# Attention over the paged cache: slots of their own for memory weights and rows, silu moved to a later step, one convolution call left out of step 0

## The chip, the cores and the metric

The kernel runs on one core of a Trainium2 chip. Its metric is the device time of one execution in microseconds (us). The core has five instruction queues that run side by side, each strictly in its own order: PE (matmuls and transposes), DVE (vector), ACT (scalar functions and copies), POOL (a second vector engine, which also issues the gathers) and SP (which issues most transfers). An instruction whose inputs or whose output slot are not ready holds up everything behind it on its queue.

## What is computed

The reference is one step of a decoder layer for a prompt of 1024 rows and for 8 samples of one token each. The stage of this change is the attention of the 8 samples over a paged cache, with other work laid between its matmuls:

```python
def mla_sample(q_nope, q_rope, c_new, kr_new, pool_ckv, pool_krope, page_table, w_uk, w_uv):
    q_lat = jnp.einsum('bthd,lhd->bthl', q_nope, w_uk)             # "absorbed" queries
    past_c = pool_ckv[page_table].reshape(Bd, -1, KV_LORA)         # 4096 cached rows per sample
    past_r = pool_krope[page_table].reshape(Bd, -1, ROPE_DIM)
    s_past = einsum('bthl,bkl->bhtk', q_lat, past_c) + einsum('bthr,bkr->bhtk', q_rope, past_r)
    ...
    p = jax.nn.softmax(s, axis=-1)
    o_lat = einsum('bhtk,bkl->bthl', p[..., :P], past_c) + einsum('bhtk,bkl->bthl', p[..., P:], c_new)

def mem_kv(mem, w_xk, w_xv):            # mem: 256 memory rows; 4 heads of 256 columns
    k = jnp.einsum('bmd,de->bme', mem, w_xk).reshape(B, M, MEM_HEADS, MEM_HEAD_DIM)
    v = jnp.einsum('bmd,de->bme', mem, w_xv).reshape(B, M, MEM_HEADS, MEM_HEAD_DIM)
    return k, v

def conv_tail(y, conv_b, g, b):         # y: causal depthwise convolution with 31 taps
    return jax.nn.silu(layer_norm(y + conv_b, g, b))
```

## The kernel before

Four stages stand ahead (projections and a gated unit, prompt attention), then comes the stage of this change, from about 404 to 680 us of the span, then the output projection, the cross attention over the memory and the feed-forward part.

The stage is a loop of 16 steps: step n works on half e = n % 2 of sample b = n // 2. A step transposes the cached rows on PE (`columns`: eight groups `trc`, then `trr` for the rotary part); the results are copied out of PSUM by ACT and DVE in turn into `ct` (the third and fourth copy of each engine belong to the second half of the groups). Then it multiplies them with the queries (`scores`, tile `main`). After an odd step the softmax of that sample runs in pieces inside the next steps (tiles `mr`, `st`, `mx`, `md`, `ma`, `E_`, `sm`, `sa`), then `values` (tile `pv`) and, behind it, the gathers of a later sample's rows by POOL. In front of all that, in step 0, `absorb` computes the absorbed queries: PE writes `tqs`, `tuk`, twice `tql`, and `tsn`, DVE copies them out as `qT`, `ukT`, `ql` and `SN`. Both `tql` use the one PSUM bank of tag `st`, so the second waits for the copy `ql` of the first. After `absorb` comes `memory_in`, which loads the 256 memory rows in four tiles `min`, transposes them (`trm`) and splits them into a high and a low part (`MH_`, `ML_`).

Three kinds of other work are laid into the steps:

- `memory_kv`: eight products of the memory rows with a head's weights (four heads, keys and values in turn), one product over an odd-even pair of steps (step 1 does a whole one). Each takes its weights in four pieces of 256 KB: a load `kraw` by SP, the high part `kwh` by POOL, the low part `kwl` by DVE, 12 matmuls `mk` on PE. Its result is copied by ACT into `ko`, and SP stores that to memory.
- `convolve`, called four times a step: each call takes `nconv` = 3 of the 62 pieces of the last convolution's DVE chain (`mix<-u,convw,mix`, L354), as long as there are any.
- `norm`, from step 6 on, and the first silu pieces, which activate the first 640 columns of the convolution's output on ACT (eight instructions in all, and the activation table has to be changed ahead of them and back to that of the exponential behind them).

Tiles live in rings of slots: a tag with bufs = 3 gives its tiles three slots in turn, and a tile waits until the last reader of the tile that had its slot is done. Before the change `kraw` and `kwl` share one ring of three; `kwh` and `ko` share one ring of two, so four `kwh` and one `ko` of a product go round it, and the slot of `ko` is taken next but one by the second `kwh` of the next product; it is free when the store of `ko` has landed. `min` has a ring of two.

The order of PE's queue in this stage is the order of the code (`manual_schedule`). The order of the other queues is set by a scheduler from the estimated times at which instructions become ready; `tc.issue_after(x)` holds instructions back until x in that order.

Of the kernel before, what the change touches and what calls it, by code (L numbers as in the profile page):

```python
# [9 lines left out]
F32 = mybir.dt.float32  # L10
F32R = mybir.dt.float32r
# [8 lines left out]
P = 128  # L20
# [5 lines left out]
NT = S + DB  # L26
# [11 lines left out]
MHD = 256  # L38
# [15 lines left out]
CONV_STEPS = 6  # L54
EARLY = 5
# [51 lines left out]
def decoder_step(ctx: ExitStack, tc: tile.TileContext, I: dict, O: dict):  # L107
# [28 lines left out]
    def cast(eng, dst, src):  # L136
        if eng == "a":
            return A.copy(dst, src)  # L138
        if eng == "v":
            return V.tensor_copy(dst, src)  # L140
        return G.tensor_scalar(dst, src, 1.0, 1.0, op0=ALU.mult, op1=ALU.mult)
# [4 lines left out]
    def split(hi, lo, src, he="a", le="v"):  # L146
        return {he: cast(he, hi, src), le: lows(le, lo, src, hi)}

    def mm3(out, lh, ll, rh, rl, start, stop, onto=False):

        T.matmul(out, lh, rh, start=start, stop=False, skip_group_check=onto)  # L151
        T.matmul(out, lh, rl, start=False, stop=False, skip_group_check=onto)  # L152
        T.matmul(out, ll, rh, start=False, stop=stop, skip_group_check=onto)  # L153
# [50 lines left out]
    with ExitStack() as c1:  # L204
# [101 lines left out]
        def glu_w(ct):  # L306
            return load_w([(G0 + ct * P, P), (G0 + CC + ct * P, P)], ct == 0)
# [5 lines left out]
        for ct in range(NCT):  # L313
            wh, wl = w_next if ct == 0 else glu_w(ct)
# [70 lines left out]
        wh, wl = load_w([(C0, LAT + RD)])  # L385
# [29 lines left out]
        for un in range(3):  # L415
            wh, wl = load_w([(un * 256, 256)])
# [40 lines left out]
    def silu(c0, c1):  # L457
        while c0 < c1:
            e = min(c1, c0 + 516)
            for k in range(NCT):  # L460
                v = mixC[:, k, c0:e]
                A.activation(v, v, AF.Silu, bias=cvec[:, 2, k:k + 1], scale=cvec[:, 1, k:k + 1])
            c0 = e


# [184 lines left out]
    with ExitStack() as c2:  # L650
        ps = Banks(tr=3, main=1, st=1, pv=1, mk=1, tl=1)
        pmp = tc.tile_pool(name="pm", bufs=1, side="left", reuse_waits="tile")
        pm = pmp.__enter__()
# [77 lines left out]
        main, probs, cts, krts, tail = {}, {}, {}, {}, {}  # L731
# [105 lines left out]
        def memory_in():  # L837
            for m in range(2):
                for g in range(2):
                    xin = pm.tile([P, 512], F32, tag="min", bufs=2, name="min")  # L840
                    nc.sync.dma_start(xin, I["mem_prompt"][0, m * P:(m + 1) * P, g * 512:(g + 1) * 512])
                    t = ps.tile([P, 4, P], F32, tag=("mk", "main", "pv", "tl")[2 * m + g], name="trm")
                    for k in range(4):
                        T.transpose(t[:, k, :], xin[:, k * P:(k + 1) * P], ident)
                    split(MH_[:, 4 * g:4 * g + 4, m * P:(m + 1) * P], ML_[:, 4 * g:4 * g + 4, m * P:(m + 1) * P], t)

        def memory_kv(h, wname, oname):

            acc = ps.tile([P, 2, MHD], F32, tag="mk", name="mk")
            for q in range(4):  # L850
                raw = pm.tile([P, 2, MHD], F32, tag="kwl", bufs=3, name="kraw")
                wh = pm.tile([P, 2, MHD], F32R, tag="kwh", bufs=2, name="kwh")
                nc.sync.dma_start(raw, I[wname][0, q * 256:(q + 1) * 256, h * MHD:(h + 1) * MHD]
                                  .rearrange("(k p) c -> p k c", p=P))
                wl = pm.tile([P, 2, MHD], F32R, tag="kwl", bufs=3, name="kwl")
                split(wh, wl, raw, "p", "v")
                if q == 2:
                    yield
                for j in range(2):
                    for m in range(2):  # L860
                        k, mc = 2 * q + j, slice(m * P, (m + 1) * P)
                        mm3(acc[:, m, :], MH_[:, k, mc], ML_[:, k, mc], wh[:, j, :], wl[:, j, :],
                            k == 0 and m == 0, k == KD - 1 and m == 1)
            o = pm.tile([P, 2, MHD], F32, tag="kwh", bufs=2, name="ko")
            cast("a", o, acc)
            nc.sync.dma_start(O[oname][0, 0, :, h, :].rearrange("(m p) d -> p m d", p=P), o)

        mkv = [(h, *n) for h in range(MH) for n in (("w_xk", "new_mem_k"), ("w_xv", "new_mem_v"))]
        def run(steps):

            for x in list(steps):
                if next(x, steps) is steps:
                    steps.remove(x)
# [6 lines left out]
        norms = [conv_norm(i, dp, ps, "tl", 2) for i in range(NTL + 1)]  # L880
        rest = conv(NCT - 1, us_[NCT - 1], S // 2)
        nconv = -(-2 * CK // (4 * CONV_STEPS))
        mem, soft, ends = memory_all(), [], []

        def norm():
            if norms and next(norms[0], norms) is norms:
                norms.pop(0)

        def convolve():
            with tc.issue_after(tail["v"].ins):  # L890
                for _ in range(nconv):
                    next(rest, None)

        with tc.manual_schedule(engines={mybir.EngineType.PE}):
            for n in range(2 * DB):
                b, e = divmod(n, 2)
                cols = columns(b, e, n < CONV_STEPS)
                next(cols, None)
                run(soft)
                next(cols, None)  # L900
                run(soft)
                run(ends)
                convolve()
                if n == 0:
                    absorb()
                    memory_in()
                else:
                    next(mem, None)
                if n == 1:
                    next(mem, None)  # L910
                if n > CONV_STEPS:
                    norm()
                run(soft)
                convolve()
                if n >= CONV_STEPS:
                    norm()
                scores(b, e)
                if n == CONV_STEPS + EARLY:
                    with tc.issue_after(tail["a"].ins):
                        silu(0, EARLY * P)  # L920
                convolve()
                if e == 0 and 0 < b < DB - 1:
                    v = values(b - 1)
                    next(v)
                    ends.append(v)
                run(soft)
                convolve()
                if e == 1:
                    soft.append(softmax(b))
                    run(soft)  # L930

            ends = [values(DB - 2)]
            run(ends)
            for _ in range(3):
                run(soft)
            run(ends)
            ends.append(values(DB - 1))
            next(ends[-1])
            run(soft)
            run(ends)  # L940
        assert not norms and not soft and not ends and next(rest, None) is None
        pmp.__exit__(None, None, None)
        rawp.__exit__(None, None, None)
        u3p.__exit__(None, None, None)
# [108 lines left out]
    with ExitStack() as c4:  # L1053
# [27 lines left out]
        with tc.issue_after(tail["sc"].ins):  # L1081
            wts, last = load_square(wp, "w_o")
        with issued_after(last):
            silu(EARLY * P, NT)
            for i in range(3, NTL):
                split_mix(i)
        gb = load_gb(pl, 1)
# [52 lines left out]
    with ExitStack() as c5:  # L1140
# [27 lines left out]
        for h in range(MH):  # L1168
            qh, qlo = (q2ab[:, 2 * h + j] if h < 2 else qx.tile([P, 2, NT], F32R, name=f"q2{j}{h}") for j in range(2))
            Q2.append((qh, qlo))  # L1170
            wh, wl = xw
# [18 lines left out]
    with ExitStack() as c6:  # L1190
# [47 lines left out]
        for h in range(MH):  # L1238
            kh, kl, vh, vl = kv
            qh, qlo = Q2[h]  # L1240
            for g in range(2):
# [25 lines left out]
                for e in range(2):  # L1267
                    o = ps.tile([P, 512], F32, tag="ov", name="ov")
# [309 lines left out]
    with ExitStack() as c9:  # L1578
# [76 lines left out]
        with tc.manual_schedule(engines={mybir.EngineType.PE, mybir.EngineType.SP}):  # L1655
            for n, (q, g, c) in enumerate(steps):
# [18 lines left out]
                if c is not None:  # L1675
# [4 lines left out]
                    if at == 2 * NGR - 2:  # L1680
                        ends = [norm_of(4), norm_of(5)]
# [36 lines left out]
```

## Time and profile before

| | |
|---|---|
| time, median of 3 runs | 1780.85 us (1779.73 to 1783.32) |
| profiled execution | 1782.63 us, its span 1780.8 us |
| busy share of the span | PE 94%, DVE 71%, ACT 35%, POOL 23% |
| granted PE clock, mean | 0.974 |
| stage of the change | 404 to 680 us |

PE is the engine that is nearly always busy; a microsecond in which PE stands still is a microsecond of the time, where nothing later takes it back. The other engines matter where PE waits for them.

### The profile page before, as it was taken

The numbers are of one execution on the slowest core, as the hardware profiler recorded it, in microseconds if no ns is written. First come the engines' busy times: TensorE is split into PE (matmuls) and PEld (weight loads), VectorE is DVE, ScalarE is ACT, GpSimd is POOL, SyncE is SP. The second block draws the span as 40 slices with busy tenths as digits, with TensorE's granted clock in tenths as the row PEclk, the third lists the DMA queues.
The fourth block names the chain that finished last, engine by engine and source line by source line (L and its number), as shares of the span: only waits on it lengthen the run. The fifth ranks groups of instructions, "written<-read, shape, count | busy, mean of one in ns | idle before, by whom it ended". The sixth has DMA issues, their size and how long they took to land.

```text
span 1780.8 us, 32063 instructions
## 1 busy us (share of the span) xinstructions
PE 1680.2 (94%) x12820; PEld 1529.6 (86%) x12820; DVE 1267.7 (71%) x2197; ACT 614.8 (35%) x1283; POOL 402.1 (23%) x456
## 2 busy tenths in 40 slices
PE   8999999997899899999999999999999899998995
PEld 8999887876677676889977879999999899998995
DVE  4899888876875547755478668887777666667666
ACT  4112177761223424111144113433333344334322
POOL 0044122241232214211046210233223110002011
PEclk9999999997999999999999999999999999999997
DMA  6121000043456443324235522344454667787644
GB/s 201 52 60 42 25 1 1 1 141 144 155 184 225 155 164 139 119 93 157 78 113 212 167 96 73 108 150 138 152 163 136 239 238 274 284 288 249 233 133 154
DMA packets 154433, 255.39 MB, mean 143 GB/s; under 512 B 12998, under 2 KB 88174, under 8 KB 150179
## 3 DMA queue, kind: packets, MB, share of 16 engines
q1 hardware_dynamic: 146939, 210.56, 35.2%
q0 software_dynamic: 7344, 42.78, 6.5%
q8 instruction: 101, 1.65, 0.4%
q14 instruction: 49, 0.40, 0.1%
HBM read 207.66 MB, written 46.11 MB: 143 GB/s over the span
## 4 chain that ended last, share of the span: by engine, by line
PE 76%; DVE 9%; DMA 7%; issue 3%; ACT 3%; POOL 1%; SPq 0%; DVEq 0%; POOLq 0%; ACTq 0%
PE pd L152 4%; PE pd L153 4%; PE pd L151 4%; PE po L151 3%; PE po L152 3%; PE po L153 3%; PE ua L151 3%; PE ua L153 3%; PE ua L152 3%; DMA ar<-in_w_down 2%; PE trc L746 2%; PE px L152 2%; PE px L151 2%; PE px L153 2%; PE ub L152 2%
## 5 line engine op out<-in xcount | busy, mean ns | idle before, releaser
L152 PE MATMUL pd<-bl,ah 128*128 128x252 f32 (+1 forms) x768 | 220.1, 287 | 10.3 <-DVE bl L144 10.1
L151 PE MATMUL pd<-bh,ah 128*128 128x252 f32 (+1 forms) x768 | 219.7, 286 | 4.9 <-ACT bh L138 4.0
L153 PE MATMUL pd<-bh,al 128*128 128x252 f32 (+1 forms) x768 | 219.1, 285 | 1.8 <-DVE al L144 1.8
L152 PEld LDWEIGHTS pd<-bl,ah 128*128 128x128 f32 x768 | 147.9, 193 | 12.2 <-DVE bl L144 12.1
L354 DVE SCALAR_TENSOR_TENSOR mix<-u,convw,mix 128x1024 f32<-128x1024 f32 (+1 forms) x150 | 154.6, 1067 | 0.2
L151 PEld LDWEIGHTS pd<-bh,ah 128*128 128x128 f32 x768 | 147.9, 193 | 5.3 <-ACT bh L138 4.2
L153 PEld LDWEIGHTS pd<-bh,al 128*128 128x128 f32 x768 | 148.0, 193 | 2.0 <-DVE al L144 2.0
L144 DVE TENSOR_TENSOR al<-ar,ah 128x1024 fp32r<-128x1024 f32 x48 | 63.7, 1326 | 72.3 <-ACT ah L138 70.1
L138 ACT CAST ah<-ar 128x1024 fp32r<-128x1024 f32 x48 | 50.3, 1049 | 159.6 <-PE pd L152 136.1
L1345 POOL TENSOR_TENSOR us<-uraw 128x512 f32<-128x512 f32 x28 | 42.8, 1548 | 232.2 <-DMA uraw<-in_w_up 136.4
L144 DVE TENSOR_TENSOR uhl<-uraw,uhl 128x512 fp32r<-128x512 f32 x50 | 50.0, 1004 | 44.9 <-ACT uhl L138 44.9
L144 DVE TENSOR_TENSOR bl<-br,bh 128x1032 fp32r<-128x1032 f32 (+2 forms) x64 | 76.3, 1194 | 7.6 <-ACT bh L138 7.6
L138 ACT CAST bh<-br 128x1032 fp32r<-128x1032 f32 (+2 forms) x64 | 60.5, 946 | 39.4 <-PE pd L153 26.0
L584 POOL TENSOR_SCALAR pr<-pr,sm 128x128 f32<-128x128 f32 (+3 forms) x64 | 47.6, 748 | 116.4 <-DVE sm L583 69.4
L746 PE MATMUL trc<-ident,craw 128*128 128x128 f32 x512 | 65.5, 281 | 7.9 <-DVE ct L140 4.5
L138 ACT CAST XHb<-tr 128x512 fp32r<-128x512 f32 x32 | 17.8, 589 | 154.5 <-PE tr L992 154.4
L746 PEld LDWEIGHTS trc<-ident,craw 128*128 128x128 f32 x512 | 57.0, 145 | 13.8 <-DVE ct L140 6.9
L1496 DVE TENSOR_TENSOR hs<-h,h 128x516 f32<-128x516 f32 x80 | 65.6, 852 | 4.3 <-DMA hc<-hs 4.2
L153 PE MATMUL ub<-XHb,uhl 128*128 128x252 f32 (+1 forms) x240 | 67.6, 282 | 0.0
L151 PE MATMUL ub<-XHb,uhl 128*128 128x252 f32 (+1 forms) x240 | 67.6, 282 | 0.0
L152 PE MATMUL ub<-XLb,uhl 128*128 128x252 f32 (+1 forms) x240 | 67.5, 281 | 0.0
L1431 POOL TENSOR_TENSOR ar<-ar,ar 128x1024 f32<-128x1024 f32 x8 | 20.2, 2523 | 197.1 <-DMA ar<-in_w_down 181.3
(550 smaller groups left out, 5743.0 us busy)
## 6 DMA issues: line engine op xcount, KB each, us to landing
ar<-in_w_down SPq DMA_DIRECT2D x96, 512.0 KB, 5.3
br<-hc SPq DMA_DIRECT2D x48, 516.0 KB, 4.5
hc<-hs SPq DMA_DIRECT2D x75, 258.0 KB, 2.1
uraw<-in_w_up SPq DMA_DIRECT2D x32, 512.0 KB, 5.9
X<-x SPq DMA_DIRECT2D x16, 512.0 KB, 2.6
kt<-in_cache_mem_k SPq DMA_DIRECT2D x32, 256.0 KB, 3.0
vsr<-in_cache_mem_v SPq DMA_DIRECT2D x32, 256.0 KB, 2.8
hc<-h SPq DMA_DIRECT2D x30, 258.0 KB, 2.4
```

The costliest lines, as they stand in the source:

```text
L138: return A.copy(dst, src)
L144: return (V if eng == "v" else G).tensor_tensor(dst, src, ff(hi), op=ALU.subtract)
L151: T.matmul(out, lh, rh, start=start, stop=False, skip_group_check=onto)
L152: T.matmul(out, lh, rl, start=False, stop=False, skip_group_check=onto)
L153: T.matmul(out, ll, rh, start=False, stop=stop, skip_group_check=onto)
L354: V.scalar_tensor_tensor(acc, x, convw[:, ct, j:j + 1], acc, op0=ALU.mult, op1=ALU.add)
L584: G.tensor_scalar(pr[:, :w], pr[:, :w], sm[:, 0:1], 1.0, op0=ALU.mult, op1=ALU.mult)
L746: T.transpose(t[:, j, :], raws[b][g // 2][:, (g % 2) * 4 + j, k * P:(k + 1) * P], ident)
L1345: G.tensor_tensor(t, x, y, op=op)
L1431: G.tensor_tensor(x, x, y, op=ALU.subtract)
L1496: V.tensor_tensor(t, hh[p, x], hh[p, y], op=op)
```

## The change

`min` gets four slots instead of two. `kraw` gets a ring of four slots of its own. `kwh` and `ko` get three slots instead of two; `kwl` keeps its three, now alone. The first of the four `convolve` calls of step 0 (ahead of `absorb`) is left out. The early silu becomes a generator with one activation per step of it, and two of its eight pieces are taken in each `convolve` call of step 13, instead of all at the end of step 11. The last `run(ends)` moves out of the block that fixes PE's order.

```diff
@@ silu
                 A.activation(v, v, AF.Silu, bias=cvec[:, 2, k:k + 1], scale=cvec[:, 1, k:k + 1])
+                yield
@@ memory_in
-                    xin = pm.tile([P, 512], F32, tag="min", bufs=2, name="min")
+                    xin = pm.tile([P, 512], F32, tag="min", bufs=4, name="min")
@@ memory_kv
-                raw = pm.tile([P, 2, MHD], F32, tag="kwl", bufs=3, name="kraw")
-                wh = pm.tile([P, 2, MHD], F32R, tag="kwh", bufs=2, name="kwh")
+                raw = pm.tile([P, 2, MHD], F32, tag="kraw", bufs=4, name="kraw")
+                wh = pm.tile([P, 2, MHD], F32R, tag="kwh", bufs=3, name="kwh")
...
-            o = pm.tile([P, 2, MHD], F32, tag="kwh", bufs=2, name="ko")
+            o = pm.tile([P, 2, MHD], F32, tag="kwh", bufs=3, name="ko")
@@ step loop
+        early = silu(0, EARLY * P)
+
         def convolve():
             with tc.issue_after(tail["v"].ins):
                 for _ in range(nconv):
                     next(rest, None)
+            if n == CONV_STEPS + EARLY + 2:
+                with tc.issue_after(tail["a"].ins):
+                    next(early, None)
+                    next(early, None)
...
-                convolve()
+                if n:
+                    convolve()
                 if n == 0:
                     absorb()
                     memory_in()
...
-                if n == CONV_STEPS + EARLY:
-                    with tc.issue_after(tail["a"].ins):
-                        silu(0, EARLY * P)
                 convolve()
...
-            run(ends)
+        run(ends)
@@ later stage
-            silu(EARLY * P, NT)
+            for _ in silu(EARLY * P, NT):
+                pass
```

PE's queue holds the same instructions in the same order as before. Three places of the other queues follow.

DVE's queue in step 0, from the copy `qT` to the second `ql`. Before:

```order
L354 SCALAR_TENSOR_TENSOR mix<-u_865,convw,mix 128x512 x3
L689 TENSOR_SCALAR qT<-tqs 96x64
...
L701 COPY ukT<-tuk 64x4x128
L144 TENSOR_TENSOR kwl<-kraw,kwh 128x512
L354 SCALAR_TENSOR_TENSOR mix<-u_865,convw,mix 128x512
L711 TENSOR_TENSOR pn<-qr,krT 32x64
...
L706 COPY ql<-tql 128x8x8
L760 COPY qrs_4833<-qr 32x8
L354 SCALAR_TENSOR_TENSOR mix<-u_865,convw,mix 128x512 x2
L710 TENSOR_TENSOR pn<-ql,cT 128x64
L354 SCALAR_TENSOR_TENSOR mix<-u_865,convw,mix 128x512
L706 COPY ql<-tql 128x8x8
```

The same place of the change:

```order
L354 SCALAR_TENSOR_TENSOR mix<-u_865,convw,mix 128x512 x3
L690 TENSOR_SCALAR qT<-tqs 96x64
...
L702 COPY ukT<-tuk 64x4x128
L354 SCALAR_TENSOR_TENSOR mix<-u_865,convw,mix 128x512
L712 TENSOR_TENSOR pn<-qr,krT 32x64
...
L707 COPY ql<-tql 128x8x8
L761 COPY qrs_4833<-qr 32x8
L711 TENSOR_TENSOR pn<-ql,cT 128x64
L144 TENSOR_TENSOR kwl<-kraw,kwh 128x512 x2
L707 COPY ql<-tql 128x8x8
```

The first `kwl` moved from ahead of the first `ql` to behind it, and there are two of them there now; the three convolution pieces between the two `ql` are gone. The five pieces ahead of `qT` (two of L356 and the three shown) stand where they stood.

DVE's queue in step 6, around the `ct` copies of the transposed rows. Before:

```order
L760 COPY qrs_4832<-qr 32x8 x4
L140 COPY ct<-trc 128x512 x2
L782 TENSOR_REDUCE mx<-st 128x8
L783 TENSOR_TENSOR mx<-mx,SN 128x8
L140 COPY ct<-trc 128x512
L144 TENSOR_TENSOR kwl<-kraw,kwh 128x512
L140 COPY ct<-trc 128x512
```

The same place of the change:

```order
L761 COPY qrs_4832<-qr 32x8 x4
L140 COPY ct<-trc 128x512 x2
L783 TENSOR_REDUCE mx<-st 128x8
L144 TENSOR_TENSOR kwl<-kraw,kwh 128x512
L784 TENSOR_TENSOR mx<-mx,SN 128x8
L140 COPY ct<-trc 128x512 x2
```

The `kwl` stands one `ct` earlier. It is that of the product's third piece now, and before that of the second: the piece whose `kwh` takes the slot of the product before's `ko`, in both kernels.

ACT's queue in steps 11 to 13, from the `ko` of step 11 on. Before:

```order
L138 COPY ko<-mk 128x512
...
L448 COPY cln<-tl 128x512
L462 ACT_TABLE_LOAD
L462 ACTIVATE mix<-mix,cvec 128x516 x4
L462 ACTIVATE mix<-mix,cvec 128x124 x4
L774 COPY mr<-main 128x512
L138 COPY ct<-trc 128x512 x4
```

In the change, around the `ko` of step 13:

```order
L138 COPY ct<-trc 128x512 x3
L462 ACT_TABLE_LOAD
L462 ACTIVATE mix<-mix,cvec 128x516 x4
L462 ACTIVATE mix<-mix,cvec 128x124 x4
L138 COPY ko<-mk 128x512
L455 COPY mix<-tl_7313 128x4x128
L448 COPY cln<-tl 128x512
L775 COPY mr<-main 128x512
```

The eight pieces stay in one row behind one table load; they moved two steps later, to between the last `ct` and the `ko` of step 13.

## Rows read from the trace of the kernel before

**Rows 1.** Windows: us, busy of PE, PEld, DVE, ACT, POOL, clock, DMA share, GB/s

```profile
412.00:432.00 20.00, 12.64 (x56) 11.40 (x54) 11.50 (x30) 1.71 (x3) 1.21 (x2) 0.50 0.26 99
432.00:436.00 4.00, 4.00 (x53) 1.71 (x52) 1.38 (x2) 0.63 (x2) 0.00 (x0) 0.78 0.09 30
...
404.00:680.00 276.00, 237.13 (x2506) 185.18 (x2505) 173.51 (x374) 82.36 (x149) 70.57 (x93) 0.92 0.46 165
```

**Rows 2.** Groups of PE, 404 to 680 us: busy, mean ns, idle before and its releasers

```profile
L151 PE MATMUL mk<-kwh,MH__4843 128*128 128x256 f32 x128 | 39.2, 307 | 1.1 <-POOL kwh L141 1.1
L152 PE MATMUL mk<-kwl,MH__4843 128*128 128x256 f32 x128 | 37.9, 296 | 1.8 <-DVE kwl L144 1.8
...
L750 PE MATMUL trr<-ident,kr 128*128 128x128 f32 x64 | 10.8, 295 | 4.6 <-DVE ct L140 4.6
...
L705 PE MATMUL tql<-qT,ukT 64*128 64x8 f32 x32 | 7.2, 359 | 5.0 <-DVE ql L706 5.0
...
L817 PE MATMUL pv<-craw,E__5338 128*8 128x256 f32 x64 | 5.3, 506 | 2.4 <-ACT E__5338 L799 2.4
...
L844 PE MATMUL trm<-ident,min 128*128 128x128 f32 x16 | 4.0, 431 | 2.0 <-DMA min<-in_mem_prompt 2.0
...
L817 PE MATMUL pv<-craw,E__6019 128*8 128x256 f32 x64 | 3.6, 379 | 0.2 <-ACT E__6019 L799 0.2
```

**Rows 3.** Timeline of DVE, step 0: start us, us, instruction, idle before and releaser

```profile
408.06 2.06 DVE L354 SCALAR_TENSOR_TENSOR mix<-u,convw,mix 128x512 f32<-128x512 f32 x3
410.05 0.21 DVE L689 TENSOR_SCALAR qT<-tqs 96x64 f32<-96x64 f32 x1
...
417.35 1.09 DVE L144 TENSOR_TENSOR kwl<-kraw,kwh 128x512 fp32r<-128x512 f32 x1 [2.24 <-POOL kwh L141]
```

**Rows 4.** Timeline of PE, step 0

```profile
410.31 1.92 PE L700 MATMUL tuk<-ident,ukn 128*64 128x128 f32 x8 [3.43 <-DVE qT L689]
...
420.73 3.58 PE L705 MATMUL tql<-qT,ukT 64*128 64x8 f32 x16 [4.99 <-DVE ql L706]
```

**Rows 5.** Timeline of POOL, step 0

```profile
416.70 1.21 POOL L141 TENSOR_SCALAR kwh<-kraw 128x512 fp32r<-128x512 f32 x2 [9.30 <-DMA kraw<-in_w_xk]
```

**Rows 6.** Timeline of all queues, end of step 7 and step 8

```profile
538.83 0.38 SPq L866 DMA_DIRECT2D out_new_mem_v<-ko  x1
...
547.66 0.62 POOL L141 TENSOR_SCALAR kwh<-kraw 128x512 fp32r<-128x512 f32 x1 [5.91 <-DMA kraw<-in_w_xk]
548.31 0.69 DVE L144 TENSOR_TENSOR kwl<-kraw,kwh 128x512 fp32r<-128x512 f32 x1 [3.31 <-POOL kwh L141]
...
549.73 0.67 PE L750 MATMUL trr<-ident,kr 128*128 128x128 f32 x2 [3.42 <-DVE ct L140]
```

**Rows 7.** Tile ko, 538 to 549 us: its store's time to landing

```profile
DMA to landing us min/median/max: 8.1/8.1/8.1
```

**Rows 8.** Timeline of all queues, step 6

```profile
518.42 0.66 PE L750 MATMUL trr<-ident,kr 128*128 128x128 f32 x4
...
519.58 0.62 POOL L141 TENSOR_SCALAR kwh<-kraw 128x512 fp32r<-128x512 f32 x1 [7.64 <-DMA kraw<-in_w_xv]
```

**Rows 9.** Timeline of ACT, steps 11 and 13

```profile
600.75 1.28 ACT L462 ACT_TABLE_LOAD   x1
602.04 4.46 ACT L462 ACTIVATE mix<-mix,cvec 128x516 f32<-128x516 f32 x8
...
627.37 0.59 ACT L138 COPY ct<-trc 128x512 f32<-128x512 f32 x1 [0.60 <-PE trc L746]
631.60 0.59 ACT L138 COPY ko<-mk 128x512 f32<-128x512 f32 x1 [3.65 <-PE mk L153]
```

**Rows 10.** Timeline of PE, steps 12 and 14

```profile
607.51 0.87 PE L746 MATMUL trc<-ident,craw 128*128 128x128 f32 x4 [3.37 <-ACT ct L138]
...
641.38 1.48 PE L746 MATMUL trc<-ident,craw 128*128 128x128 f32 x8 [2.58 <-DVE ct L140]
```

**Rows 11.** Tile kraw, 599 to 608 us: time to landing of the load seen there

```profile
DMA to landing us min/median/max: 2.7/2.7/2.7
```

More of the change, by code (lines that the diff above doesn't have):

```diff
@@ L939, in decoder_step @@
             run(soft)
-            run(ends)
-        assert not norms and not soft and not ends and next(rest, None) is None
+        run(ends)
+        assert not norms and not soft and not ends and next(rest, None) is None and next(early, None) is None
         pmp.__exit__(None, None, None)
```

## The prediction

> **What bounds the kernel now.** I read the windows first, then the groups of PE with what ended the idle time before them, then the timelines of the queues that those name. PE sets the time: in the stage of the change it is busy 237.1 of 276 us [rows 1], so 38.9 us are all that better waits can give here, plus what the clock takes. The clock is the second thing to see: from 412 to 432 us, where PE waits again and again and else runs the narrow matmuls of `absorb`, the granted clock is 0.50, the 1.2 GHz level, and it is still at a mean of 0.78 from 432 to 436 us, with PE busy throughout [rows 1]. The same 64 matmuls `pv` take 5.3 us behind a wait of 2.4 us and 3.6 us elsewhere [rows 2], so a wait of two to three microseconds costs up to 1.7 us more, by the clock.
>
> PE's waits in this stage fall in three kinds. In step 0 it waits 3.43 us for `qT` and 4.99 us for `ql` [rows 4] and 2.0 us for the memory rows [rows 2]. In step 1 it waits 1.1 + 1.8 us for weight pieces and in step 2, ahead of the first `pv`, 2.4 us for `E_` [rows 2]. In the even steps from 8 on it waits for copies of transposed rows: 3.42 us in step 8 [rows 6], 1.2 us in step 10 (the rest of the 4.6 us of `trr` in rows 2), 3.37 us in step 12 and 2.58 us in step 14 [rows 10].
>
> **Step 0: the two terms of the head.** The 4.99 us for `ql` come from DVE's order: `kwl` stands ahead of `ql`, waits 2.24 us for its `kwh` and runs 1.09 us [rows 3]. In the change it stands behind. The gain is 2.24 + 1.09 = 3.3 us. The wait of 3.43 us for `qT` stays: DVE reaches `qT` only after five convolution pieces, the last three at 0.69 us each [rows 3], and the order of the change has the same five ahead of it, although one call less is made; the three pieces that went are those behind `ql`. So the third part of the change, taken by its words, does nothing there. The four slots of `min` let all four loads go out at once, and the 2.0 us wait between the second and third transpose group [rows 2] goes: 2.0 us. PE then runs without a gap from the second `tql` on, and the clock, at 0.78 in the mean from 432 to 436 us, should be up before the first scores. At a mean of 0.78 a share of 0.44 of the four microseconds ran at half speed, 1.8 us, worth 0.9 us at full speed; I take 0.6 us (0 to 0.9).
>
> Does the moved `kwl` hold up the second `ql` instead? Its two `kwh` started at 416.70 us, when the load landed [rows 5]. Now two more row tiles and two more weight pieces, 1.05 MB, go out with them. Nothing in the trace shows their landing. At the 99 GB/s that the window behind moved [rows 1] they would take 10 us; at best, by the 2.7 us in which a single load lands elsewhere [rows 11], they come with the others. I take 2.6 us for the last of them, nearer the lone load since the window's DMA share of 0.26 shows free engines, and half of it for the first two pieces, so that two `kwl` run between 418 and 421 us; the second `tql` starts 3.3 us earlier than at 420.73 us and takes 3.58 us [rows 4], so `ql` is wanted at 421.0 us. It fits, narrowly.
>
> **Steps 1 to 5.** The next loads are far ahead, so `mk` no longer waits: 1.1 + 1.8 = 2.9 us (1.8 if DVE, with its convolution pieces, cannot follow). One `kwl` less stands ahead of `E_`, which is 0.7 us by its own time and 0.5 us of waiting; I take 1.2 us off the 2.4 us, and with a wait that short the clock holds: 1.7 us more [rows 2]. Together 2.9 us (0 to 4.1). The three pieces left out of step 0 come later, 3 x 0.69 = 2.1 us of DVE; two of them fall ahead of `E_` in step 4 and I charge 0.7 us (0 to 2.1). The rest falls where DVE waits for PE.
>
> **Even steps 6 to 14: what does not go.** The stall of step 8 looks like a late load, but the `kwh` that ends it waits for two transfers: its own `kraw` and, because it takes the slot of `ko`, the store. The store goes out at 538.83 us [rows 6] and lands 8.1 us later [rows 7], at 546.9 us; `kwh` starts at 547.66 us, `kwl` follows at 548.31 us, and the copies that PE waits for stand behind it on DVE [rows 6]. With slots of its own the load is early, yet the store still has to land: three slots hand the slot of `ko` to the third piece instead of the second, and the order of step 6 puts that piece's `kwl` ahead of both copies of the second half. So step 8 keeps its wait, 0.3 us shorter (`kwh` started 0.7 us after the store's landing, and one reduction more stands ahead of the copy); step 10 the same, 0.6 us for both. Step 6 gains a wait that it did not have: PE begins `trr` at 518.42 us without waiting, while `kwh` starts at 519.58 us [rows 8]. Take 0.5 us off for the load and add the 2.07 us that lie between the starts of `kwh` and `trr` in step 8 [rows 6]: `trr` starts at about 521.15 us, 2.7 us late, less 0.2 us of another wait that goes. The clock may fall with it, 1.3 us (0 to 1.7). I charge 3.8 us (0 to 5).
>
> **Silu.** In step 11 it holds ACT from 600.75 to 606.5 us and PE waits 3.37 us for the copy behind it [rows 9, 10], with a fall of the clock of 1.7 us as for `pv`. In step 12 the wait for the store's piece then shows; I take 0.65 us, half of step 10's. Gain 3.37 + 1.7 - 0.65 = 4.4 us. In step 13 ACT is free from 627.96 us to the `ko` at 631.60 us; load and pieces take 1.28 + 4.46 = 5.74 us [rows 9], so `ko`, its store and two copies are 2.1 us late. That reaches step 14, whose wait of 2.58 us is already the store's; but the store goes out when the gather is nearly over. I take 0 (from -2.2 to +0.8). The Trainium skill (ScalarE: Activation LUTs, What ACT_TABLE_LOAD costs) gives 1.28 us for the load and about 1.38 us for a drain with every switch. By that rule the `ko` of step 13 would be 3.5 us late and the sum up to 1.4 us smaller. The trace agrees on the load and shows no drain behind it: the first piece starts 0.01 us after the load's end [rows 9].
>
> **The end.** `ob` stands ahead of one 0.2 us product now: 0.2 us.
>
> **Sum.** 3.3 + 2.0 + 0.6 + 2.9 + 2.9 - 0.7 - 3.8 + 0.6 + 4.4 + 0 + 0.2 = 12.4 us. The profiled execution took 1782.63 us, 1.8 us above the median of the runs; 1782.6 - 12.4 = 1770.2 us, as a median 1768.5 us. Its own bounds are 1764 to 1774 us.
>
> **Rivals.**
>
> *Late first loads.* The eight loads share the engines with the last gathers; if the second of the two `kwl` ends near 427 us instead of 421, the second `ql` gives all of it back. Then 3.3 + 2.0 + 0.6 = 5.9 us go: 1774.4 us. For it speaks that POOL had waited 9.30 us for the first piece as it is [rows 5]; against it that DMA was at 0.26 of its time from 412 us on [rows 1].
>
> *DVE as the bound of the first six steps.* DVE has the same 62 pieces to do. If it, not PE, paces steps 1 to 5, what the head gains is lost to waits for `ct` and `mx`, and `E_` comes no earlier: 5.9 + 2.9 us less, 1777.2 us. Against it: from 412 to 432 us DVE was busy 11.5 of 20 us [rows 1], so it has room to begin earlier too.
>
> *The store lands later (the other side).* Behind each store SP now issues two loads at once instead of one, in the same window as the gathers. Each microsecond that the store lands later is one at five even steps, and steps 10 and 12 would lose the clock too, 3.4 us. 5x + 3.4 = 12.4 gives x = 1.8 us as the point from which the change loses; at 3 us it is 6 us slower, 1786.9 us. Against it: the store is issued ahead of those loads.
>
> *The store's wait goes.* If the 8.1 us were the load's doing, the store could land as a lone load does, in 2.7 us [rows 11]. Then step 6 loses nothing (3.8), step 8 gains 3.42 + 1.7 (4.8 more than charged), step 10 0.9 and step 12 0.65 more: 22.5 us, 1758.3 us. The Trainium skill (DMA: Bandwidth & Descriptors, Anatomy of one DMA) has a fit of 2.0 us plus the bytes at 436 GB/s for one transfer, by which the 256 KB of the store would be an estimated 2.6 us. The store's own row has 8.1 us, among gathers [rows 7], and it decides.
>
> **How the numbers follow.** Forecast 0.55, late loads 0.12, DVE the bound 0.11, late store 0.10, no store wait 0.10, something else 0.02. The range 1758 to 1778 us leaves out the late store and little more. A measurement of this kernel tells about 0.2% (3.6 us) from no change. Faster by more than that is the forecast, late loads, no store wait and half of DVE the bound: 0.82. Within it the other half and the milder late stores: 0.10. Slower 0.08.
>
> **What would show it.** In the profile after: the first wait of `tuk` for `qT` still near 3.4 us; the second `tql` with a wait under 2 us, `trm` with none; the clock at its upper level before the first `main`; no wait of `mk` for `kwl`; a new wait of `trr` for `ct` in step 6 and the one of step 8 still above 2.5 us, with `kwh` starting just as the store of `ko` lands; no wait for ACT in step 12 and a `ko` of step 13 about 2 us behind its matmuls. The prediction is wrong if the even steps show no wait for the store, or if DVE's waits in steps 1 to 5 grow by what the head gave.

## The result, and the profile after

The changed kernel takes 1769.69 us in the median of 8 runs (1763.73 to 1774.98), the kernel before 1780.53 us (8 runs, 1778.52 to 1786.51): a ratio of 0.9932, interval 0.9916 to 0.9948. The forecast was 1768.5 us (1758 to 1778). The profiled execution took 1770.1 us, 12.5 us less than that of before; the sum had 12.4 us. That the total fits so well does not mean that its terms do, as the rows show.

The windows of the stage, in the columns of [rows 1]:

```profile
412.00:432.00 20.00, 17.99 (x129) 15.88 (x128) 13.02 (x32) 3.84 (x7) 2.33 (x3) 0.64 0.44 159
432.00:436.00 4.00, 4.00 (x37) 4.00 (x36) 3.70 (x6) 0.85 (x2) 1.62 (x2) 1.00 0.14 25
404.00:680.00 276.00, 247.66 (x2561) 194.71 (x2559) 185.33 (x383) 90.31 (x161) 78.39 (x98) 0.94 0.50 184
```

From 412 to 432 us PE is busy 18.0 us instead of 12.6, and from 432 to 436 us the clock is at its upper level, where the kernel before had 0.78. Below is PE's timeline, with the idle time before each row and what ended it:

```profile
410.38 1.91 PE L701 MATMUL tuk<-ident,ukn 128*64 128x128 f32 x8 [3.42 <-DVE qT L690]
417.45 3.58 PE L706 MATMUL tql<-qT,ukT 64*128 64x8 f32 x16 [1.64 <-DVE ql L707]
...
447.32 2.82 PE L747 MATMUL trc<-ident,craw 128*128 128x128 f32 x12 [2.21 <-DVE ct L140]
...
458.56 3.64 PE L818 MATMUL pv<-craw,E__5335 128*8 128x256 f32 x64 [1.18 <-ACT E__5335 L800]
...
477.40 2.81 PE L747 MATMUL trc<-ident,craw 128*128 128x128 f32 x12 [1.67 <-DVE ct L140]
482.86 0.27 PE L787 MATMUL st<-ident,mx 128*8 128x128 f32 x1 [1.82 <-DVE mx L784]
491.94 3.64 PE L818 MATMUL pv<-craw,E__5682 128*8 128x256 f32 x64 [1.44 <-ACT E__5682 L800]
...
512.62 0.66 PE L751 MATMUL trr<-ident,kr 128*128 128x128 f32 x4 [0.84 <-DVE ct L140]
526.35 0.66 PE L747 MATMUL trc<-ident,craw 128*128 128x128 f32 x4 [1.32 <-ACT ct L138]
...
627.38 2.29 PE L747 MATMUL trc<-ident,craw 128*128 128x128 f32 x16 [0.70 <-DVE ct L140]
```

The kernel before, in the same places of steps 2 and 4:

```profile
455.80 1.53 PE L746 MATMUL trc<-ident,craw 128*128 128x128 f32 x12 [0.82 <-DVE ct L140]
486.50 1.09 PE L746 MATMUL trc<-ident,craw 128*128 128x128 f32 x8 [0.69 <-DVE ct L140]
492.19 0.38 PE L786 MATMUL st<-ident,mx 128*8 128x128 f32 x1 [3.10 <-DVE mx L783]
```

Read it against [rows 2, 4, 6, 10]. The wait for `qT` is what it was. The one for `ql` fell from 4.99 to 1.64 us, and those of `trm` and `mk` are gone. The first `pv` waits 1.18 us and takes 3.64 us instead of 5.33. Against that stand longer waits for DVE's copies `ct` in steps 2 and 4 (2.21 and 1.67 us, before 0.82 and 0.69; the one for `mx` is shorter), one of 1.44 us for `E_` in step 5, and a new kind, for ACT's copies in the odd steps from 7 on (here 1.32 us; with the shorter waits behind it, 5.6 us over steps 7 to 13). The waits of `trr` in steps 8 and 10 are gone, and step 6 has one of 0.84 us where 2.7 were forecast.

The loads, the store and `kwh` around step 8, and ACT in steps 7 and 13, from the timelines of those queues:

```profile
506.83 9.81 SPq L854 DMA_DIRECT2D kraw<-in_w_xk  x4
534.01 0.38 SPq L867 DMA_DIRECT2D out_new_mem_v<-ko  x1
537.29 0.72 POOL L141 TENSOR_SCALAR kwh<-kraw 128x512 fp32r<-128x512 f32 x1 [0.36 <-DMA out_new_mem_v<-ko]
...
525.45 0.36 ACT L138 COPY ob<-pv 8x256 f32<-8x256 f32 x1 [7.35 <-PE trc L747]
...
616.73 1.28 ACT L462 ACT_TABLE_LOAD   x1
618.02 4.47 ACT L462 ACTIVATE mix<-mix,cvec 128x516 f32<-128x516 f32 x8
622.40 0.56 ACT L138 COPY ko<-mk 128x512 f32<-128x512 f32 x1
```

The four loads now leave some 20 us ahead of their use. `kwh` of step 8 still waits for the store, as forecast, but starts 3.3 us after the store's issue instead of 8.8 [rows 6].

The starts of ACT's eight `ko`, one in each odd step, cut the stage into pieces. From them, and from PE's first `tqs` and last `pv` (`pv<-summ,ob`), the table gives what each piece got shorter, in us. The second pair is one more execution of each kernel, from the experiments below.

| piece | forecast | first pair | second pair |
|---|---|---|---|
| steps 0 and 1, to the first `ko` | 3.3 + 2.0 + 0.6 + 2.9 = 8.8 | 44.27 - 34.32 = 9.95 | 44.00 - 34.61 = 9.4 |
| steps 2 to 5 | 2.9 - 0.7 = 2.2 | 62.20 - 65.33 = -3.1 | 64.35 - 64.75 = -0.4 |
| steps 6 and 7 | -3.8 | 26.90 - 28.83 = -1.9 | 27.25 - 27.49 = -0.2 |
| steps 8 and 9 | 0.3 | 32.37 - 28.50 = 3.9 | 29.63 - 30.18 = -0.6 |
| steps 10 and 11 | 0.3 | 28.58 - 29.25 = -0.7 | 28.54 - 28.39 = 0.2 |
| steps 12 to 15 | 4.4 | 60.03 - 54.49 = 5.5 | 58.04 - 53.63 = 4.4 |
| the rest of the stage | 0.2 | 0.0 | -0.7 |
| sum | 12.4 | 13.6 | 12.1 |

The head and the silu are the gain, in both pairs. The steps between them gave nothing: -1.8 and -1.0 us, forecast -1.0, but made of other parts: too much was expected of steps 2 to 5, and too much was charged to step 6. So the sum is right by luck.

### The profile page after: what moved, and what is told of

It reads as the page before. It is cut to its first block, busy times and chain, and to the rows that moved or that the text cites. A ratio compares the mean times of both kernels' runs of the same rounds, so it can differ in the third digit from the quotient of the medians.

```text
span 1768.0 us, 32067 instructions
## 1 busy us (share of the span) xinstructions
PE 1675.8 (95%) x12820; PEld 1527.7 (86%) x12820; DVE 1262.3 (71%) x2197; ACT 613.4 (35%) x1283; POOL 407.2 (23%) x456
## 4 chain that ended last, share of the span: by engine, by line
PE 53%; DVE 4%; DMA 3%; issue 2%; POOL 1%; ACT 1%; SPq 0%; DVEq 0%; POOLq 0%; ACTq 0%
PE pd L152 5%; PE pd L151 4%; PE pd L153 4%; PE po L151 3%; PE po L152 3%; PE po L153 3%; PE ua L151 3%; PE ua L153 3%; PE ua L152 3%; PE px L152 2%; PE px L151 2%; PE px L153 2%; PE ub L152 2%; PE ub L151 2%; PE ub L153 2%
## 5 line engine op out<-in xcount | busy, mean ns | idle before, releaser
L152 PEld LDWEIGHTS pd<-bl,ah 128*128 128x128 f32 x768 | 149.2, 194 | 11.4 <-DVE bl L144 11.3
```

## The experiments

There were three sets of runs, each on one chip (the first has before at 1781.91 us, the second at 1780.14, the third at 1775.31); a ratio is to the kernel before in its set. The changed kernel itself was not run in the third set.

**The parts one by one.** Each is the kernel before with one part of the change: the slots alone (`min` 4, a ring `kraw` of 4, `kwh` and `ko` 3), the silu alone (with the moved `run(ends)`), the left-out call alone.

> The kernel before with the memory slots alone (four for the rows, a ring of four for kraw, three for kwh and ko); silu and the convolution as before. By the terms of the prediction: 12.4 less the 4.4 of the silu, without the 0.7 for later convolution pieces, about 8.7 us, so 1772 us, with a wait of trr of 2.7 us or more left in step 8 and the wait of 3.4 us for ACT's copy still in step 12. If instead the late load was what step 8 waited for, the waits of trr in steps 6 and 8 are under 1 us together, about 14 us are gained in the stage before the odd steps give some of it back, and the silu's 3.4 us stay: 1767 to 1774 us. The trace tells the two apart, not the time.

> The kernel before with the silu's early pieces moved from step 11 to step 13, and nothing else. By the prediction's term: the wait of 3.4 us for ACT's copy in step 12 goes, with 1.7 us of clock, and 0.65 us come back as a wait for the weight piece; step 14 keeps 2.6 us: 4.4 us gained, 1776 us. A rival: the ko of step 13 is 2.1 us late, step 14 waits about 2 us more, and the gain is 2 us or less, 1778 to 1780 us.

> The kernel before with one call of the convolution left out of step 0, and nothing else. By the prediction: the wait of tuk for qT stays at 3.4 us, since the five pieces ahead of it are the same; the second ql comes no earlier, since kwl ahead of it waits for its load anyway; 0 to 0.7 us lost by later pieces: 1780 to 1782 us, the same within the error. The rival (the words of the change): qT comes up to 3.4 us earlier and the kernel is 3 us faster, 1777 us.

Measured, beside 1781.91 us for before: the slots 1772.69 us, ratio 0.996 (0.9944 to 0.9975); the silu 1777.69 us, 0.9981 (0.9966 to 0.9995); the call 1779.1 us, 0.9995 (0.9978 to 1.0012). By the ratios these are 7.1, 3.4 and 0.9 us, together 11.4, where the ratio of the whole change is worth 12.1 us and the sum had 8.7, 4.4 and 0 to -0.7. The gains add. From PE's timelines: with the slots alone step 12 keeps its wait for ACT's copy, and `trr` waits 0.62 us in step 6 and not at all in step 8, as the rival has it and not the forecast; with the silu alone step 12's wait is gone and 0.48 us of `trr` come back (forecast 0.65); with the call alone `qT` is as late as ever.

```profile
600.11 1.11 PE L746 MATMUL trc<-ident,craw 128*128 128x128 f32 x4 [3.37 <-ACT ct L138]
```

```profile
410.06 1.92 PE L700 MATMUL tuk<-ident,ukn 128*64 128x128 f32 x8 [3.43 <-DVE qT L689]
```

**The loads alone.**

```diff
-                raw = pm.tile([P, 2, MHD], F32, tag="kwl", bufs=3, name="kraw")
+                raw = pm.tile([P, 2, MHD], F32, tag="kraw", bufs=4, name="kraw")
```

> The kernel before with one edit: kraw in a ring of its own of four slots. kwh and ko keep their ring of two, so the second kwh of a product still takes the slot of ko and waits for its store, while the loads go out ahead of the store. The prediction's theory (the store lands 8.1 us after its issue and that is the stall of step 8): trr still waits 3 us or more in step 8 and 1 us in step 10, kwh starts 8 us behind the issue of the store, time 1776 to 1781 us. The rival (the load, queued behind the store on SP and slow among the gathers, was the wait): kwh starts within 3.5 us of the issue of the store, trr waits under 1 us in steps 8 and 10, time 1768 to 1775 us.

Measured: 1778.35 us, ratio 0.9984 (0.9965 to 1.0003). `trr` has no wait in steps 8 and 10, as the rival wants; the store goes out at 538.94 us and `kwh` starts 5.2 us later, between the two theories; and the time is in the forecast's range. Timelines of SP and POOL:

```profile
538.94 0.38 SPq L866 DMA_DIRECT2D out_new_mem_v<-ko  x1
...
544.10 0.62 POOL L141 TENSOR_SCALAR kwh<-kraw 128x512 fp32r<-128x512 f32 x1 [2.24 <-ACT ct L138]
```

This run by itself settled nothing, because two runs in which step 8 had not been touched (silu alone, call alone) also had at most 0.74 us of wait in it. So both kernels were profiled once more.

**Both kernels again.**

> The kernel before once more, unchanged, to see which rows of its one profiled execution repeat. If they belong to the program: tql waits 5.0 us for ql, trr 3.4 us in step 8 and 1.2 us in step 10, and no odd step waits for a copy of ACT, all within 0.3 us. If they belong to that execution (the runs with only the silu or only the convolution changed, whose step 8 is the same code, show under 1 us there and 0.4 to 1.3 us for ACT in the odd steps): tql 2.3 to 3.8 us, trr under 1 us in step 8, ACT's copies 0.4 us or more late in most odd steps.

> The changed kernel once more beside the others, for its ratio on this chip and to see whether its waits for ACT's copies in steps 7, 9, 11 and 13 (1.3, 0.4, 1.3, 1.3 us) and for DVE's in steps 2 and 4 (2.2, 1.7 us) repeat. If they belong to the program: the same within 0.2 us. If to the execution: they move by more than 0.5 us in at least two of the steps. Time 1766 to 1773 us.

Measured in the second set: before again 1781.07 us, ratio 1.0004 (0.9988 to 1.0021); the change again 1766.06 us, 0.9931 (0.9911 to 0.9951). Rows of the kernel before, from the timelines of PE, SP, POOL and ACT:

```profile
419.05 3.58 PE L705 MATMUL tql<-qT,ukT 64*128 64x8 f32 x16 [2.98 <-DVE ql L706]
549.55 0.66 PE L750 MATMUL trr<-ident,kr 128*128 128x128 f32 x4 [0.67 <-DVE ct L140]
...
541.39 0.38 SPq L866 DMA_DIRECT2D out_new_mem_v<-ko  x1
547.47 0.62 POOL L141 TENSOR_SCALAR kwh<-kraw 128x512 fp32r<-128x512 f32 x1 [3.16 <-DMA kraw<-in_w_xk]
...
532.14 0.36 ACT L138 COPY ob<-pv 8x256 f32<-8x256 f32 x1 [5.23 <-PE trc L746]
```

and of the changed kernel, SP, POOL and ACT:

```profile
532.98 0.38 SPq L867 DMA_DIRECT2D out_new_mem_v<-ko  x1
539.12 0.63 POOL L141 TENSOR_SCALAR kwh<-kraw 128x512 fp32r<-128x512 f32 x1 [3.22 <-DMA out_new_mem_v<-ko]
...
523.77 0.36 ACT L138 COPY ob<-pv 8x256 f32<-8x256 f32 x1 [5.86 <-PE st L806]
```

Three readings follow. First, `qT`'s wait, those of `trm` and `mk`, and step 12's 3.37 us repeat to a tenth or two; the wait for `ql` (4.99, 2.98), step 8's (3.42, 0.67) and step 10's (1.19, 0) do not. In the changed kernel the wait for `ct` in step 2 repeats (2.21 us), the one in step 4 is 1.13 us. Second, the late copies of ACT in the odd steps are in the kernel before as well, so the change did not make them. Third, in the changed kernel `kwh` of step 8 starts 6.1 us after the store's issue although its load left long before: the store is what it waits for, and here `trr` waits 0.99 us for it.

**The convolution truly behind `absorb`.**

```diff
-                V.tensor_copy(ql[:, k].rearrange("p b h -> p h b"), t)
+                tail["v"] = V.tensor_copy(ql[:, k].rearrange("p b h -> p h b"), t)
```

> The changed kernel, with the convolution pieces of step 0 held behind the copy ql on DVE, which is what the third part of the change says and does not do. If the pieces ahead of qT are what tuk waits for: its wait falls from 3.4 us to under 0.7 us, the clock is up earlier, and the seven pieces run between 418 and 432 us, where DVE is idle half the time: 3 to 4.5 us gained, 1766 us or 0.2% under the changed kernel. The rival, DVE as the bound of steps 1 to 4: the step 0 is shorter by the same 3 us, but the waits for ct and mx in steps 2 and 4 grow by 2 us or more, and the gain is 1 us or less.

Measured in the second set, beside the change again (1766.06 us): 1764.67 us, ratio 0.9927 (0.9908 to 0.9945), not to be told from it. The wait for `qT` goes; a new one for `ML_` takes 2.31 us, since DVE now runs pieces between its copies. PE's timeline:

```profile
406.91 1.06 PE L701 MATMUL tuk<-ident,ukn 128*64 128x128 f32 x8 [0.49 <-DVE qT L690]
...
423.69 3.24 PE L766 MATMUL main<-ct,qst 128*32 128x512 f32 x16 [2.31 <-DVE ML__4844 L144]
```

The first `ko` is 33.37 us behind `tqs` instead of 34.61: 1.2 us of 3. The time is the rival's, its sign is not there: the waits for `ct` and `mx` in steps 2 and 4 are 2.21, 1.12 and 3.22 us, where the repeat of the change has 2.21, 1.13 and 3.20. Most of what `qT` gave was lost in step 0 itself, to `ML_`.

**DVE without the convolution.**

```diff
-            with tc.issue_after(tail["v"].ins):
-                for _ in range(nconv):
-                    next(rest, None)
+            if n == 0:
+                with tc.issue_after(tail["v"].ins):
+                    for _ in range(nconv):
+                        next(rest, None)
...
```

> The changed kernel, with the convolution pieces of steps 1 to 5 left out (the last channels of the convolution stay incomplete, so its output is not the reference's). If DVE with its pieces is the bound of steps 1 to 4: the waits of trc for ct in steps 2 and 4 (2.2 and 1.1 to 1.7 us), of st for mx in step 4 (1.8 to 3.2 us) and of pv for E_ (1.2 and 0.4 to 1.4 us) fall to under 1.5 us together, 6 us or more less with the clock: under 1762 us. If they come from the order of DVE's queue or from PE's copies: more than half of them stay, 1765 us or more.

Measured in the third set: 1751.21 us, ratio 0.9862 (0.9837 to 0.9886). Windows from first to third `ko` (nearly), of this kernel and then of the changed one:

```profile
440.00:491.00 51.00, 49.77 (x599) 39.88 (x602) 26.65 (x67) 15.22 (x29) 14.47 (x19) 1.00 0.57 206
```

```profile
440.00:504.50 64.50, 55.11 (x594) 43.56 (x590) 55.36 (x110) 14.55 (x27) 19.46 (x18) 0.92 0.46 166
```

In the changed kernel DVE is busy 55.4 of 64.5 us; without the pieces it is 26.7 of 51, the clock never falls, and of the waits in steps 2 and 4 only 1.23 us (`mx`) are left. DVE was the bound of steps 2 to 5, at a price of 65.3 - 50.9 = 14.4 us between the first and the third `ko`; the next kernel, of the same set, has 65.0 there. The same run shows the store's wait of the forecast, in steps 6, 8, 10 and 12: `trr` waits 1.60, 1.07, 0.56 and 0.80 us. Timelines of SP, POOL and PE:

```profile
491.61 0.38 SPq L867 DMA_DIRECT2D out_new_mem_k<-ko  x1
497.74 0.62 POOL L141 TENSOR_SCALAR kwh<-kraw 128x512 fp32r<-128x512 f32 x1 [6.13 <-DMA out_new_mem_k<-ko]
499.81 0.66 PE L751 MATMUL trr<-ident,kr 128*128 128x128 f32 x4 [1.60 <-DVE ct L140]
...
527.85 0.65 PE L751 MATMUL trr<-ident,kr 128*128 128x128 f32 x4 [1.07 <-DVE ct L140]
```

**`ko` in its own ring.**

```diff
-            o = pm.tile([P, 2, MHD], F32, tag="kwh", bufs=3, name="ko")
+            o = pm.tile([P, 2, MHD], F32, tag="ko", bufs=2, name="ko")
```

> The changed kernel, with ko in a ring of its own of two slots, so that no kwh waits for a store. The prediction's theory (the third kwh waits for a store that lands 8.1 us after its issue): the wait of trr in step 6 (0.84 and 0.35 us in two runs of the changed kernel) and the one in step 8 (0 and 0.99 us) go, and kwh starts earlier by 2 us or more in the even steps. If the store lands within 3.5 us and the wait is DVE's: trr still waits 0.3 to 0.9 us in step 6, time within 2 us of the changed kernel.

Measured in the third set: 1760.04 us, ratio 0.9911 (0.9889 to 0.9934), which is not distinguishable from the change's 0.9932. No `trr` waits in steps 6 to 12. But `kwh` does not start earlier, as was expected: in step 8 it starts 9.7 us behind the store's issue, because now PE's `mk` holds its slot. What changed is the order on DVE, where its `kwl` stands behind all four `ct` of the step. Two kernels of this set that keep the shared ring (late rows and both, below) have that order too and no such wait, although their `kwh` starts 8.4 to 9.9 us behind the store's issue in steps 6 to 12, later than in the changed kernel. Step 8 of the late rows, timelines of SP, POOL and DVE:

```profile
528.75 0.38 SPq L872 DMA_DIRECT2D out_new_mem_v<-ko  x1
538.63 1.21 POOL L141 TENSOR_SCALAR kwh<-kraw 128x512 fp32r<-128x512 f32 x2 [6.97 <-DMA out_new_mem_v<-ko]
...
536.27 0.69 DVE L140 COPY ct<-trc 128x512 f32<-128x512 f32 x1 [0.21 <-PE trc L747]
539.28 1.69 DVE L144 TENSOR_TENSOR kwl<-kraw,kwh 128x512 fp32r<-128x512 f32 x2 [1.83 <-POOL kwh L141]
```

The kernel without the convolution has the `kwl` ahead of two `ct`, as the changed kernel has, and waits. So the store's wait is real, and what it costs PE is set by what stands behind that `kwl` on DVE: nothing in three kernels of this set, 4.0 us over four steps in the fourth.

**The late copies of the odd steps.** ACT's `ob` should start 3.7 us after the first of the 64 `pv`. In the changed kernel it starts 5.75 us (step 7: 519.70 to 525.45 us) or 4.25 us (the repeat) after it, and DVE's `sa`, which needs the matmul behind `pv`, is late with it: what PE has finished is seen late. First all gathers, the rotary rows' too, were put behind `ob`:

```diff
-            if b + 2 < DB:
-                gather(b + 2)
...
+            if b + 2 < DB:
+                hold = dp.tile([H, 1], F32, tag="hold", bufs=2, name="hold")
+                with tc.issue_after(cast("p", hold, ob[:H, 0:1]).ins):
+                    gather(b + 2)
...
```

> The changed kernel, with the gathers of the cached rows behind the copies ob (a one-column copy on POOL waits for ob), and the rotary rows' gather behind the other four. In the changed kernel ACT's ob starts 1.0 to 2.5 us after the last of the 64 pv matmuls has begun in steps 5 to 13, where it is 0.45 us in steps 3 of all runs. If POOL's issue of gathers beside the matmuls is what holds the signals of PE back: ob 0.45 us after it in every step, no wait for ACT's copies, 5 us less of PE's idle time, 1765 us. If not: ob stays late by 0.5 to 2 us. Rows then land about 3 us later; if the next sample's columns have to wait for them the kernel is slower.

Measured in the second set: 1772.02 us, ratio 0.9961 (0.9944 to 0.9977). ACT's `ob` starts 3.70 us after `pv` in every step and no copy of ACT is late, but `trr` now waits for the rotary rows. Timelines of ACT and PE:

```profile
523.89 0.36 ACT L138 COPY ob<-pv 8x256 f32<-8x256 f32 x1 [5.30 <-PE pv L821]
...
511.64 1.09 PE L754 MATMUL trr<-ident,kr 128*128 128x128 f32 x4 [2.72 <-DMA kr<-in_cache_krope,idx]
```

Then only the four gathers of the cached rows were moved, alone and together with the convolution behind `ql`:

```diff
-                gather(b + 2)
+                gather_rope(b + 2)
...
+                with tc.issue_after(cast("p", hold, ob[:H, 0:1]).ins):
+                    for c in range(4):
+                        gather_part(ra if b % 2 == 0 else dp, b + 2, c)
```

> The changed kernel, with the four gathers of a sample's cached rows held behind ob by a one-column copy on POOL, and the rotary rows' gather left where the changed kernel has it. If the signals of PE are held back by POOL's gathers beside the matmuls, as the run with all gathers late suggests: ob 0.45 us after the last pv matmul in every step, no wait for ACT's copies in steps 7 to 13, trr without a wait for the rotary rows, 3 to 5 us less than the changed kernel: about 1764 us. The rival: the rows themselves land too late, or kwh behind the later gathers holds up kwl and the copies on DVE, and trr or trc wait 1 us or more in the even steps: 1767 to 1772 us.

> Late rows and the convolution pieces behind ql together. If each acts in its own steps (0 and 5 to 13), the gains add: 1.5 to 3 us of the second and 3 to 5 us of the first, 1760 to 1763 us. If the late rows cost what they give: as the run behind_ql, 1765 us.

Measured in the third set: late rows 1759.58 us, ratio 0.9907 (0.989 to 0.9924); both 1753.24 us, 0.9874 (0.9855 to 0.9893). No copy of ACT is late in either. But none is late in the kernels with `ko`'s own ring and without the convolution, which gather as the changed kernel does, in this set. ACT's row of step 7 with the own ring, 3.70 us after its `pv` at 518.04 us:

```profile
521.74 0.36 ACT L138 COPY ob<-pv 8x256 f32<-8x256 f32 x1 [5.30 <-PE pv L818]
```

So the late rows have nothing to win there, and 0.9907 is no better than the own ring's 0.9911. What the two edits together add over the late rows, 6.3 us, is the convolution behind `ql`, more than the 2 us by which the stage got shorter in the profiles (249.4 to 247.4 us); the rest is not explained. This version is faster than the kernel before, and its interval lies below that of the change. That comparison is across sets, though, and the late copies, which the third set does not have, may weigh in it; within the set it is 6.3 us faster than the late rows.

## Why the prediction was right in sum, point by point

- **The sum: right by luck.** By the table, steps 2 to 5 came out 5.3 and 2.6 us worse than their terms, and steps 6 and 7 came out 1.9 and 3.6 us better. The head and the silu are within 1.2 us of theirs.
- **Step 0 and the clock: right in sum, two terms mis-sized.** The two `kwl` were forecast between 418 and 421 us and ran from 418.63 to 420.92 us, just ahead of the second `ql` at 421.06 us, so the first loads were not late. The second `tql` waits 1.64 us and `trm` none; the first `ko` is 9.9 and 9.4 us earlier (forecast 8.8). The wait for `ql` was taken from an execution at the high end: 2.98 us in the repeat and 2.29 and 2.73 us with the call or the silu alone, against 4.99. So its term of 3.3 us is 1.3 us in the second pair. The clock, put at 0.6 us (0 to 0.9), made up for it: PE is busy 30.59 us before and 28.70 us after with the same 218 matmuls from `tqs` to the first `ko`, 32.23 and 29.00 us in the second pair, which is 1.9 and 3.2 us.
- **The third part of the change: right.** `qT` waits 3.42 us; the call is worth nothing that the runs can tell.
- **Steps 1 to 5: wrong.** "One `kwl` less stands ahead of `E_`" came true (1.2 us and the clock), and was taken back, in both pairs, by the waits for `ct`. The step that failed is "I charge 0.7 us": 2.2 us were forecast for steps 2 to 5 and -3.1 and -0.4 measured. PE stands still 1.0 and 0.6 us more there; the other 2 us of the first pair are clock (a mean of 0.90 instead of 0.95 in steps 4 and 5). This is the rival with DVE as the bound, for these steps alone; the run without the pieces shows it.
- **Step 6: right in kind, wrong in size.** "The store goes out at 538.83 us and lands 8.1 us later" was one execution's figure for step 8, taken for all. From the issue of the store to the start of the `kwh` that waits for it, step 8 has 8.8 us there, 6.1 in its repeat, 5.2 with the loads alone, 3.3 and 6.1 in the changed kernel and 6.2 without the convolution. In step 6 of the changed kernel it is 5.4 and 4.9 us, where the forecast's working has 7.2. By that working, which ends at a wait of 2.7 us, 1.8 and 2.3 us less leave 0.9 and 0.4 us; 0.84 and 0.35 us were there, and the clock held, for the 3.8 charged. So the mechanism held, and its size was off. The sign "the one of step 8 still above 2.5 us" failed too, with 0 and 0.99 us. By the fit that the Trainium skill (DMA: Bandwidth & Descriptors, Anatomy of one DMA) gives for transfers issued by GpSimd, the store, which SP issues, would be an estimated 2.6 us; the one store whose landing the changed kernel's trace shows, that of step 1, has 2.2 us, those waited for in steps 6 to 12 do not agree.
- **Steps 8 and 10: the gain there was chance.** The 3.9 us that the first pair shows are -0.6 in the second.
- **Odd steps: not foreseen.** The changed kernel's profile has 5.6 us of waits for late signals in steps 7 to 13, its repeat 3.1 us; the page of before had none, its repeat has 4.2 us. In the first pair they take back what steps 8 and 10 gained; in the second both kernels have them.
- **Silu: right.** 4.4 us forecast, 5.5 and 4.4 us in the profiles, 3.4 us by the runs of that part alone. `ko` of step 13 starts at 622.40 us, 2.1 us behind the end of its matmuls, as forecast, and step 14 did not mind. The first piece starts 0.01 us behind the table's load of 1.28 us: of the drain that the Trainium skill (ScalarE: Activation LUTs, What ACT_TABLE_LOAD costs) adds to each switch, this trace too shows nothing behind the load.

## What to carry to other kernels

A landing time that is the same at its minimum, median and maximum is one event: profile the unchanged kernel twice before a term rests on a transfer's wait, and keep the waits that repeat. An instruction that waits for a transfer costs only what stands behind it on its queue, so look at its place there as well as at its slot. When a load is taken off an engine's path, ask which engine is next full in those steps; here DVE was busy 61.6 of 71 us (440 to 511 us) before anything was changed. Where words of a change and the order of its instructions differ, the order is what runs. Making it do what the words say was worth 6.3 us in one set, and nothing that the runs can tell in another.

## What the hardware showed that was not expected

PE's finished work can be seen late by the other queues. In one execution `ob` started 2.1 us late on ACT, while PE's own records run on without a gap, and DVE and POOL were late with it. In the first two sets it came in most steps from 5 on in all seven kernels whose gathers run beside `pv`, and not in the one execution whose gathers run behind `ob`. In the third set it came in no step, though two kernels there gather beside `pv` as well, and the first profile of the kernel before does not have it. That points to the gathers without showing that they are the cause, and what decides whether it occurs stays open.

A store of 256 KB among the gathers has no fixed time from its own issue, but nearly one from the last gather of cached rows ahead of it. In the 26 places of steps 6 to 12 where a profile names the store as what `kwh` waited for, `kwh` starts 3.3 to 9.9 us behind the store's issue and 11.6 to 14.0 us behind that gather's. The two kernels with late rows and the one with all gathers late, whose store goes out 3.3 to 4.1 us behind the gather, wait 8.4 to 9.9 us; the changed kernel, whose store goes out 7.9 to 8.3 us behind it, 3.3 to 6.1 us. So moving the gathers nearer to the store moved `kwh` back by as much.

The late copies fit in here: they hold up PE, and so the store, behind the gathers. Where the `kwl` that waits stands ahead of `ct`, the waits of PE for `ct` behind it sum to 4.6 and 4.0 us over steps 6 to 12 in the two executions without late copies (the first of the kernel before, and the one without the convolution), and to 0 to 1.4 us in the eight with them. This link is read from the rows; no run changed the late copies alone.
